# 1/rms on ScalarE and GpSimd in a two-layer encoder: ln and exp with one Newton step in place of three Newton steps on VectorE

## The chip, the core and the metric

The kernel runs on one core of a Trainium2 chip. The core has five engines that run side by side, each through its own instructions in order: TensorE (PE, matrix products, results in PSUM), VectorE (DVE), ScalarE (ACT), GpSimd (POOL) and SyncE (SP, which here issues most DMAs). They meet at semaphores only. The metric is the device time of one execution in microseconds (us), the median of several runs.

## The reference

Two layers, each with four groups of attention heads beside each other, an output projection, and an MLP with squared ReLU; 1024 tokens, model width 1024, all in float32. What matters here is every place that divides by a root mean square:

```python
def rms_norm(x, g):
    y = x * lax.rsqrt(jnp.mean(x * x, axis=-1, keepdims=True) + EPS)
    return y * g
...
for l in range(DEPTH):
    h = rms_norm(x, norm1_g[l])                 # before the input projection
    ...
    q = rms_norm(cq, q_norm_g) @ w_uq           # group A: latents of 192 and
    c = rms_norm(ckv, kv_norm_g)                #   of 128 columns
    w = p[:, :, 0] - lam * p[:, :, 1]           # group B: difference of two softmaxes
    o = rms_norm(o, subln_g)                    #   norm of each head's output
    mix = concat([rms_norm(y_a), y_b, rms_norm(y_c), rms_norm(y_d)])
    x = x + mix @ w_out[l]
    h = rms_norm(x, norm2_g[l])
    x = x + jnp.square(relu(h @ w_up[l])) @ w_down[l]
return rms_norm(x, final_norm_g)
```

Group C also adds a sink, exp(sink − max), to each softmax denominator.

## The kernel before, in words

Activations lie transposed: a tile has 128 features in its partitions and tokens along its rows, so a token's sum of squares runs over partitions. Each float32 product is made of three passes over rounded halves (`wh`, `wl` for weights; `xh`, `xl`, `far` for activations): lines 220 to 222. ACT writes the high half (L194), DVE or POOL the low one by subtraction (L188, the helper `tt`, which records every elementwise operation of two tensors).

A norm works like this. ACT squares, DVE sums tiles, PE multiplies by ones (L261), which puts the sums of 128 tokens into one PSUM column, so 1024 tokens are a tile of 128x8. `rstd_cols` scales it and adds EPS (`ms`, L263), `rsqrt_cols` makes 1/rms of it (`rs_r`, with `rs_t` as scratch): an integer guess (L247) and three Newton steps of three small DVE operations each (L249, L188, L251), ten operations in a row that each need the one before. The columns go back into rows either by products with the identity (`spread_here`, L297) or by a PE transpose (L270), a copy (L272), a store to DRAM (`drows`) and a broadcast load (`rows_of`, `spread`).

The order of one layer: input projection of group B's columns; attention B (`attn_b`) with the projections of A's latents and of group D woven in; attention D with the projection of C and `latent_up`; attention C; attention A with parts of the output projection; the MLP (`mlp_up`, `mlp_down`). A norm that isn't needed at once is a tail, a generator that `tick` advances by a step between steps of the main work. `proj_latent` (L664 on) collects sums of squares of the latents in `sq0` to `sq2`, and at its end makes two 1/rms, one after the other, in the middle of attention B. `attn_b` softmaxes two score tiles for each block of queries: `p` is read out of PSUM by a custom DVE operation with a running maximum `nm` (L809), ACT takes the exponential (L812); then the coefficient `cb` = z0 · (−lambda) / z1 (L893, L894) scales the second tile (ACT, L896), POOL adds the two, PE transposes the sum (L843) and multiplies it with v (L831, L832). `sub_norm` is B's norm, `mix_group` that of D, C and A, `final` the last one, run for each half of the tokens.

Instructions are put in order by a scheduler that goes by its own model of durations; in the MLP, PE's order alone is the code's.

Of the kernel before, what the change touches and what calls it, by code (L numbers as in the profile page):

```python
# [15 lines left out]
I32 = mybir.dt.int32  # L16
AF = mybir.ActivationFunctionType
ALU = mybir.AluOpType
# [127 lines left out]
class Trunk:  # L146
# [94 lines left out]
    def rsqrt_cols(self, ms):  # L241

        nc = self.nc
        n = ms.shape[1]
        r = self.cp.tile([P, n], F, tag="rs_r", name="rs_r")
        t = self.cp.tile([P, n], F, tag="rs_t", name="rs_t")
        nc.vector.tensor_scalar(r.bitcast(I32), ms.bitcast(I32), -0.5, 1597463007.0, ALU.mult, ALU.add)  # L247
        for _ in range(3):
            nc.vector.scalar_tensor_tensor(out=t, in0=r, scalar=-0.5, in1=r, op0=ALU.mult, op1=ALU.mult)  # L249
            self.tt(t, t, ms)  # L250
            nc.vector.scalar_tensor_tensor(out=r, in0=t, scalar=1.5, in1=r, op0=ALU.add, op1=ALU.mult)  # L251
        return r

    def rstd_cols(self, sq, count, rhs, tag="mm"):

        nc = self.nc
        g = rhs.shape[1]
        n = sq.shape[1] // P
        ps = self.bank(tag, [P, n * g])
        for t in range(n):  # L260
            nc.tensor.matmul(ps[:, t * g:(t + 1) * g], sq[:, t * P:(t + 1) * P], rhs, start=True, stop=True)  # L261
        ms = self.cp.tile([P, n * g], F, tag="ms", name="ms")
        nc.vector.tensor_scalar(ms, ps, 1.0 / count, EPS, ALU.mult, ALU.add)  # L263
        return self.rsqrt_cols(ms)
# [36 lines left out]
    def setup(self):  # L301
        nc, d = self.nc, self.d
        tile = lambda shape, name, dt=F: self.const.tile(shape, dt, name=name)
# [360 lines left out]
    def proj_latent(self, l, one, xs, rb, tabs, lat, krd, rows_out):  # L664
# [3 lines left out]
        squares = [self.col("sq%d" % i, 8) for i in range(3)]  # L668
# [20 lines left out]
        self.tt(q, q, squares[1], ALU.add)  # L689
        for m, count in ((q, 192), (k, 128)):  # L690
            nc.vector.tensor_scalar(m, m, 1.0 / count, EPS, ALU.mult, ALU.add)
            rows_out.append(self.rows_of(self.rsqrt_cols(m)))
# [175 lines left out]
    def attn_b(self, l, t, qb, kb, vb, out):  # L868
# [3 lines left out]
        def head(h2):  # L872
# [15 lines left out]
            def probs(qt):  # L888
                ps = []
                for c in range(2):  # L890
# [3 lines left out]
                nc.vector.scalar_tensor_tensor(out=c, in0=z[0][:, qt:qt + 1], scalar=self.nlam[:, l:l + 1], in1=c,  # L894
                                               op0=ALU.mult, op1=ALU.mult)
# [12 lines left out]
    def sub_norm(self, y, rz, out):  # L908
# [6 lines left out]
        r = self.rstd_cols(sq, 64, self.pairs)  # L915
# [150 lines left out]
    def attn_c(self, l, qc, kc, vc, ys):  # L1066
# [3 lines left out]
        for kv in range(2):  # L1070
# [6 lines left out]
            for g in range(2):  # L1077
# [16 lines left out]
                self.tt(z, z, es, ALU.add)  # L1094
# [21 lines left out]
    def mix_group(self, mix, k0, ys, g, eng=None):  # L1116
# [3 lines left out]
        r = self.rstd_cols(acc, 256, self.ones[:, 0:1])  # L1120
# [373 lines left out]
```

## Time and profile before

| | |
|---|---|
| runs of the kernel, us | 2724.05, 2724.58, 2730.74 (median 2724.58) |
| profiled execution: its span, us (the page gives no other time of it) | 2735.0 |
| mean granted PE clock in it | 0.966 of full speed |
| 1/rms in a run | 20, so 200 small operations on DVE |
| tables loaded by ACT | 1, at the start, 1.28 us |
| exponentials of dense attention (L812) | 192, mean 1147 ns |

A profile is one execution recorded instruction by instruction. Its page gives busy time for each engine; a list of waits says which instruction stood idle until which other one had ended; the timeline shows single instructions. A row reads: line of the code, engine, operation, tile written <- tiles read, shape and type. Times in a timeline are from the span's start. "PEld" is TensorE's loading of weights, which overlaps its products. A window's row gives the time of each engine in that stretch, the granted clock, the DMA engines' busy share and GB/s.

### The profile page before, as it was taken

How to read it: one execution, taken by the hardware profiler on the slowest of the kernel's cores; microseconds unless marked ns; L12 is line 12 of the kernel's file. 1: busy time of each engine (PE TensorE's matmuls, PEld its weight loads, DVE VectorE, ACT ScalarE, POOL GpSimd, SP SyncE). 2: the span in 40 equal slices, each digit the busy share in tenths (PEclk: the TensorE clock that was granted, in tenths of full speed). 3: DMA queues.
4: the chain of work that ended last, by engine and by line, in shares of the span. 5: the costliest groups of instructions: out<-in, count | busy, mean ns of one | idle time of the engine just before them, and what ended most of it. 6: DMA issues, size and time to landing. Idle time of an engine off the chain costs nothing.

```text
span 2735.0 us, 37689 instructions
## 1 busy us (share of the span) xinstructions
PE 2559.4 (94%) x12298; PEld 2112.1 (77%) x12298; DVE 2006.5 (73%) x3560; ACT 1434.5 (52%) x2555; POOL 1138.4 (42%) x762
## 2 busy tenths in 40 slices
PE   8989988999899999999999899799998999999997
PEld 6778866787678887888877687677876788878886
DVE  7787767884966769778567777588749666688776
ACT  4667756673534445444427676566735444444444
POOL 2555641201345554555435556322013455545552
PEclk9989999999999999999998899999999999999998
DMA  5534597322144457444254335963221444664431
GB/s 173 168 103 128 155 272 227 105 88 74 35 147 146 158 181 254 151 131 128 94 160 120 110 113 157 273 218 86 78 70 34 159 159 145 219 222 150 138 101 62
DMA packets 191667, 389.19 MB, mean 142 GB/s; under 512 B 23840, under 2 KB 33008, under 8 KB 191472
## 3 DMA queue, kind: packets, MB, share of 16 engines
q1 hardware_dynamic: 177648, 361.62, 43.1%
q10 hardware_dynamic: 13824, 25.17, 2.6%
q8 instruction: 97, 1.59, 0.2%
q14 instruction: 98, 0.80, 0.1%
HBM read 263.29 MB, written 123.41 MB: 141 GB/s over the span
## 4 chain that ended last, share of the span: by engine, by line
PE 68%; DVE 14%; DMA 7%; ACT 4%; issue 4%; POOL 1%; SPq 0%; DVEq 0%; ACTq 0%; POOLq 0%
PE u L220 8%; PE u L222 8%; PE u L221 8%; PE mm L220 5%; PE p L220 5%; PE p L221 5%; PE p L222 5%; PE mm L221 5%; PE mm L222 5%; PE sb L807 3%; DVE p L809 2%; DVE part L188 2%; PE tr L843 2%; ACT p L812 2%; DVE ptl L188 1%
## 5 line engine op out<-in xcount | busy, mean ns | idle before, releaser
L188 POOL TENSOR_TENSOR wl<-raw,wh 128x512 fp32r<-128x512 f32 x448 | 638.2, 1425 | 703.7 <-ACT wh L194 681.5
L194 ACT ACTIVATE wh<-raw 128x512 fp32r<-128x512 f32 x448 | 281.4, 629 | 580.6 <-PE u L221 317.9
L188 POOL TENSOR_TENSOR wl<-ws,wh 128x512 fp32r<-128x512 f32 (+1 forms) x120 | 150.5, 1256 | 473.4 <-ACT wh L194 465.5
L220 PE MATMUL u<-far,wh 128*128 128x512 f32 x768 | 302.3, 394 | 8.1 <-ACT ev L1240 5.9
L188 DVE TENSOR_TENSOR raw<-raw 128x512 f32<-128x512 f32 x256 | 227.5, 894 | 103.8 <-DMA raw<-in_w_up 51.8
L222 PE MATMUL u<-far,wl 128*128 128x512 f32 x768 | 301.2, 392 | 2.7 <-POOL wl L188 2.7
L221 PE MATMUL u<-far,wh 128*128 128x512 f32 x768 | 301.6, 393 | 0.2 <-DVE far L188 0.2
L188 DVE TENSOR_TENSOR ptl<-tr,pth 128x512 fp32r<-128x512 f32 (+2 forms) x384 | 238.4, 628 | 70.2 <-ACT pth L194 69.1
L812 ACT ACTIVATE p<-p,nm 128x1024 f32<-128x1024 f32 x192 | 220.2, 1147 | 97.6 <-DVE nm L809 95.1
L194 ACT ACTIVATE pth<-tr 128x512 fp32r<-128x512 f32 (+2 forms) x384 | 205.5, 547 | 117.7 <-PE tr L843 67.1
L220 PE MATMUL p<-far,wh 128*128 128x512 f32 x640 | 253.0, 395 | 8.0 <-DVE ev L188 8.0
L222 PE MATMUL p<-far,wl 128*128 128x512 f32 x640 | 252.0, 394 | 1.2 <-POOL wl L188 1.2
L221 PE MATMUL p<-far,wh 128*128 128x512 f32 x640 | 252.1, 394 | 0.0
L807 PE MATMUL sb<-stack 96*128 96x512 f32 x640 | 219.8, 426 | 26.4 <-DVE nm L809 25.7
L188 DVE TENSOR_TENSOR far<-act,far 128x512 fp32r<-128x512 f32 x224 | 205.4, 946 | 14.6 <-ACT far L194 14.6
L188 POOL TENSOR_TENSOR p<-p 128x1024 f32<-128x1024 f32 x64 | 154.4, 2416 | 143.8 <-ACT p L896 130.4
L220 PEld LDWEIGHTS u<-far,wh 128*128 128x128 f32 x768 | 145.9, 190 | 40.6 <-ACT ev L1240 7.2
L222 PEld LDWEIGHTS u<-far,wl 128*128 128x128 f32 x768 | 145.8, 190 | 34.2 <-POOL wl L188 3.5
L220 PE MATMUL mm<-xh,wh 128*128 128x512 f32 x416 | 170.6, 410 | 0.9 <-DVE both L188 0.5
L221 PEld LDWEIGHTS u<-far,wh 128*128 128x128 f32 x768 | 145.7, 190 | 30.9 <-DVE far L188 0.5
L222 PE MATMUL mm<-xh,wl 128*128 128x512 f32 x416 | 167.9, 404 | 0.1
L221 PE MATMUL mm<-xl,wh 128*128 128x512 f32 x416 | 167.6, 403 | 0.0
(243 smaller groups left out, 6141.2 us busy)
## 6 DMA issues: line engine op xcount, KB each, us to landing
act<-acts SPq DMA_DIRECT2D x224, 256.0 KB
raw<-in_w_up SPq DMA_DIRECT2D x128, 256.0 KB
acts<-ev SPq DMA_DIRECT2D x128, 256.0 KB
raw<-in_w_down SPq DMA_DIRECT2D x128, 256.0 KB
acts<-ev ACTq DMA_DIRECT2D x96, 256.0 KB
ws<-in_w_in SPq DMA_DIRECT2D x76, 256.0 KB
rz<-drows SPq DMA_DIRECT2D x40, 256.0 KB
stack<-kd SPq DMA_DIRECT2D x32, 256.0 KB
```

The source lines that it names most:

```text
L188: (eng or self.nc.vector).tensor_tensor(out=out, in0=a, in1=b, op=op)
L194: nc.scalar.activation(hi, src, AF.Copy)
L220: mm(ps, w[0], x[0][:, sl], start=start, stop=False)
L221: mm(ps, w[0], x[1][:, sl], start=False, stop=False)
L222: mm(ps, w[1], x[0][:, sl], start=False, stop=stop)
L807: self.nc.tensor.matmul(ps, q[:, qt * P:(qt + 1) * P], k[:, sl], start=i == 0, stop=i == len(passes) - 1)
L809: self.nc.vector.tensor_tensor_reduce(out=p[:, sl], in0=ps, in1=self.zero[:, 0:1].bitcast(F).broadcast_to([P, 512]), scale=-scale, scalar= ...
L812: self.nc.scalar.activation(p, p, AF.Exp, bias=nm[:, 1:2], scale=-1.0, accum_out=z)
L843: nc.tensor.transpose(t[:, k * 256 + i * P:k * 256 + (i + 1) * P], p[:, (j * 2 + k) * P:(j * 2 + k + 1) * P], self.ident)
```

## The change

`rsqrt_cols` takes the logarithm and exp(−0.5 · ln) on ACT and then one Newton step, on the engine that is asked for: DVE (three operations), or POOL (four, since it has them in another form). POOL is asked for in `sub_norm`, in the mix norms of D and C, and for the latents; DVE stays for the first norm of a layer, A's mix norm, the MLP's norm and the final one. The latents' two sums stand in one tile of 128x16, summed and scaled by POOL, with one 1/rms, one transpose and one store. B's coefficient becomes a TENSOR_SCALAR with one tensor and two per-partition scalars. In attention C, POOL adds the sink to z. A set of ACT's tables that has ln and exp is named at the start.

```diff
-    def rsqrt_cols(self, ms):
+    def rsqrt_cols(self, ms, eng=None):
         r = self.cp.tile([P, n], F, tag="rs_r", name="rs_r")
         t = self.cp.tile([P, n], F, tag="rs_t", name="rs_t")
-        nc.vector.tensor_scalar(r.bitcast(I32), ms.bitcast(I32), -0.5, 1597463007.0, ALU.mult, ALU.add)
-        for _ in range(3):
-            nc.vector.scalar_tensor_tensor(out=t, in0=r, scalar=-0.5, in1=r, op0=ALU.mult, op1=ALU.mult)
-            self.tt(t, t, ms)
-            nc.vector.scalar_tensor_tensor(out=r, in0=t, scalar=1.5, in1=r, op0=ALU.add, op1=ALU.mult)
+        nc.scalar.activation(r, ms, AF.Ln)
+        nc.scalar.activation(r, r, AF.Exp, scale=-0.5)
+        if eng is not None:
+            self.tt(t, r, r, eng=eng)
+            self.tt(t, t, ms, eng=eng)
+            eng.tensor_scalar(t, t, -0.5, 1.5, ALU.mult, ALU.add)
+            self.tt(r, r, t, eng=eng)
+            return r
+        nc.vector.scalar_tensor_tensor(out=t, in0=r, scalar=-0.5, in1=r, op0=ALU.mult, op1=ALU.mult)
+        self.tt(t, t, ms)
+        nc.vector.scalar_tensor_tensor(out=r, in0=t, scalar=1.5, in1=r, op0=ALU.add, op1=ALU.mult)
         return r
...
     def setup(self):
+        nc.scalar.preload_act_table_set("natural_log_exp_and_others")
...
     def proj_latent(...):
-        squares = [self.col("sq%d" % i, 8) for i in range(3)]
+        ms, more = self.col("sq0", 16), self.col("sq1", 8)
+        squares = [ms[:, 0:8], more, ms[:, 8:16]]
...
-        self.tt(q, q, squares[1], ALU.add)
+        self.tt(q, q, more, ALU.add, nc.gpsimd)
         for m, count in ((q, 192), (k, 128)):
-            nc.vector.tensor_scalar(m, m, 1.0 / count, EPS, ALU.mult, ALU.add)
-            rows_out.append(self.rows_of(self.rsqrt_cols(m)))
+            nc.gpsimd.tensor_scalar(m, m, 1.0 / count, EPS, ALU.mult, ALU.add)
+        both = self.rows_of(self.rsqrt_cols(ms, nc.gpsimd))
+        rows_out.extend([both[0:8], both[8:16]])
...
     def attn_b(...):
-                nc.vector.scalar_tensor_tensor(out=c, in0=z[0][:, qt:qt + 1], scalar=self.nlam[:, l:l + 1], in1=c,
-                                               op0=ALU.mult, op1=ALU.mult)
+                nc.vector.tensor_scalar(c, c, z[0][:, qt:qt + 1], self.nlam[:, l:l + 1], ALU.mult, ALU.mult)
...
     def sub_norm(...):
-        r = self.rstd_cols(sq, 64, self.pairs)
+        r = self.rstd_cols(sq, 64, self.pairs, eng=nc.gpsimd)
...
     def attn_c(...):
-                self.tt(z, z, es, ALU.add)
+                self.tt(z, z, es, ALU.add, nc.gpsimd)
...
     def mix_group(...):
-        r = self.rstd_cols(acc, 256, self.ones[:, 0:1])
+        r = self.rstd_cols(acc, 256, self.ones[:, 0:1], eng=None if eng else self.nc.gpsimd)
```

The scheduler orders attention anew: of PE's 12,092 products about 960 stand elsewhere, all in attention; in the MLP PE's order is the same. Lines of the new kernel differ from the old by −1 at first and by up to +8 later (L809 is L817, L812 is L820, L896 is L903).

First place: DVE in attention B of layer 0, where the latents' sums are complete. The rows `ISA p,nm` are the softmax reads of a score tile, `sq_829` and `sq_831` the sums, `rs_r` the two 1/rms. Before:

```order
L272 COPY rows<-mm 8x128
L893 RECIPROCAL cb<-z_1388 128x1
L188 TENSOR_TENSOR sq_829<-sq_829,sq_830 128x8
L894 SCALAR_TENSOR_TENSOR cb<-z_1387,nlam,cb 128x1
L809 ISA p,nm<-sb,zero 128x512
L809 ISA nm 128x1
L691 TENSOR_SCALAR sq_829<-sq_829 128x8
L809 ISA p,nm<-sb,zero,nm 128x512
L809 ISA nm 128x1
L247 TENSOR_SCALAR rs_r<-sq_829 128x8
L247 TENSOR_SCALAR rs_r<-sq_831 128x8
```

and at the same place now:

```order
L277 COPY rows<-mm 8x128
L901 RECIPROCAL cb<-z_1383 128x1
L902 TENSOR_SCALAR cb<-cb,z_1382,nlam 128x1
L817 ISA p,nm<-sb,zero 128x512
L817 ISA nm 128x1
L817 ISA p,nm<-sb,zero,nm 128x512
L817 ISA nm 128x1
L197 SCALAR_TENSOR_TENSOR both<-part,par,both 64x512
L817 ISA p,nm<-sb,zero 128x512
```

The sums, their scaling and the chain of both 1/rms are gone from between the softmax reads. They are now on POOL, between its additions of the two softmaxes (`p<-p`), the tables of the rotation (`tabc`, `tabs`) and low halves (`both`); before, its rows there were

```order
L188 TENSOR_TENSOR tabc<-tabc,rb 128x1024
L188 TENSOR_TENSOR tabs<-tabs,rb 128x1024
L188 TENSOR_TENSOR p<-p 128x1024
L188 TENSOR_TENSOR both<-part,both 48x512
L188 TENSOR_TENSOR p<-p 128x1024 x2
```

and now they are

```order
L187 TENSOR_TENSOR tabc<-tabc,rb 128x1024
L187 TENSOR_TENSOR sq_825<-sq_825,sq_826 128x8
L187 TENSOR_TENSOR tabs<-tabs,rb 128x1024
L187 TENSOR_TENSOR p<-p 128x1024
L187 TENSOR_TENSOR both<-part,both 48x512
L698 TENSOR_SCALAR sq_825<-sq_825 128x8
L187 TENSOR_TENSOR p<-p 128x1024
L187 TENSOR_TENSOR rs_t<-rs_r 128x16
L187 TENSOR_TENSOR rs_t<-rs_t,sq_825 128x16
L251 TENSOR_SCALAR rs_t<-rs_t 128x16
L187 TENSOR_TENSOR rs_r<-rs_r,rs_t 128x16
```

Between the scaling and the four Newton operations stand ACT's ln and exp; in ACT's order they are placed among exponentials (L820) and high halves of transposed softmaxes (`pth`):

```order
L820 ACTIVATE p,z_1382<-p,nm 128x1024
L903 ACTIVATE p<-p,cb 128x1024
L193 ACTIVATE pth<-tr 128x512 x2
L246 ACTIVATE rs_r<-sq_825 128x16
L820 ACTIVATE p,z_1383<-p,nm 128x1024
L757 ACTIVATE pvt<-pv 64x512
L247 ACTIVATE rs_r<-rs_r 128x16
```

On PE, the transpose of the joined norms stands at row 567 of its order; before, the two transposes stood at row 558, and what now lies ahead of it besides is 14 transposes of `p`, 3 products of scores and 5 products with v.

Second place: DVE at the norm of layer 0's MLP, where `raw` are sums of weight blocks and `far` low halves of activations. Before:

```order
L263 TENSOR_SCALAR ms<-mm 128x8
L247 TENSOR_SCALAR rs_r<-ms 128x8
L249 SCALAR_TENSOR_TENSOR rs_t<-rs_r 128x8
L188 TENSOR_TENSOR raw<-raw 128x512
L188 TENSOR_TENSOR rs_t<-rs_t,ms 128x8
L198 SCALAR_TENSOR_TENSOR far<-x_7141,par,far 128x512
L188 TENSOR_TENSOR raw<-raw 128x512
L251 SCALAR_TENSOR_TENSOR rs_r<-rs_t,rs_r 128x8
L249 SCALAR_TENSOR_TENSOR rs_t<-rs_r 128x8
L188 TENSOR_TENSOR rs_t<-rs_t,ms 128x8
```

and now:

```order
L268 TENSOR_SCALAR ms<-mm 128x8
L187 TENSOR_TENSOR raw<-raw 128x512
L197 SCALAR_TENSOR_TENSOR far<-x_7093,par,far 128x512
L254 SCALAR_TENSOR_TENSOR rs_t<-rs_r 128x8
L187 TENSOR_TENSOR raw<-raw 128x512
L187 TENSOR_TENSOR rs_t<-rs_t,ms 128x8
L256 SCALAR_TENSOR_TENSOR rs_r<-rs_t,rs_r 128x8
```

The guess and two of three steps are gone; the same two `raw` and one `far` stand among what is left.

Third place: ACT at the first half of the final norm, where L1455 squares a block of x and L1456 scales it; ln and exp are new there:

```order
L1456 ACTIVATE x_19775<-x_19775,par 128x512
L1455 ACTIVATE ev<-x_19856 128x512
L246 ACTIVATE rs_r<-ms 128x4
L1456 ACTIVATE x_19856<-x_19856,par 128x512
L247 ACTIVATE rs_r<-rs_r 128x4
L193 ACTIVATE wh<-raw 128x512
```

ln stands behind a square and exp behind a scaling of x. In the second half nothing stands between or behind them.

More of the change, by code (lines that the diff above doesn't have):

```diff
@@ L15 @@
 R = mybir.dt.float32r
-I32 = mybir.dt.int32
 AF = mybir.ActivationFunctionType
@@ L246, in rsqrt_cols, with rstd_cols @@
         t = self.cp.tile([P, n], F, tag="rs_t", name="rs_t")
-        nc.vector.tensor_scalar(r.bitcast(I32), ms.bitcast(I32), -0.5, 1597463007.0, ALU.mult, ALU.add)
-        for _ in range(3):
-            nc.vector.scalar_tensor_tensor(out=t, in0=r, scalar=-0.5, in1=r, op0=ALU.mult, op1=ALU.mult)
-            self.tt(t, t, ms)
-            nc.vector.scalar_tensor_tensor(out=r, in0=t, scalar=1.5, in1=r, op0=ALU.add, op1=ALU.mult)
+        nc.scalar.activation(r, ms, AF.Ln)
[9 more added lines that the diff above has]
+        nc.vector.scalar_tensor_tensor(out=r, in0=t, scalar=1.5, in1=r, op0=ALU.add, op1=ALU.mult)
         return r
-    def rstd_cols(self, sq, count, rhs, tag="mm"):
+    def rstd_cols(self, sq, count, rhs, tag="mm", eng=None):
         nc = self.nc
@@ L263, in rstd_cols @@
         nc.vector.tensor_scalar(ms, ps, 1.0 / count, EPS, ALU.mult, ALU.add)
-        return self.rsqrt_cols(ms)
+        return self.rsqrt_cols(ms, eng)
     def rows_of(self, col, grid=False):
```

## The prediction

> **What bounds the kernel now.** I read the page's busy shares first.
>
> ```profile
> PE 2559.4 (94%) x12298; PEld 2112.1 (77%) x12298; DVE 2006.5 (73%) x3560; ACT 1434.5 (52%) x2555; POOL 1138.4 (42%) x762
> ```
>
> TensorE (PE) is the bound, 94% busy; what a change can win is its idle time, 175.6 us (2735.0 less 2559.4), and the time it runs below full clock. So the second view is the list of waits, for PE alone. Columns: total us, times, longest.
>
> ```profile
> PE sb L807 <- DVE nm L809: 25.7, 23, 5.4
> ...
> PE mm L297 <- DVE rs_r L251: 6.4, 2, 4.1
> ...
> PE u L297 <- DVE rs_r L251: 5.7, 2, 3.5
> ...
> PE mm L270 <- DVE rs_r L251: 3.2, 3, 2.0
> ```
>
> Three of these rows wait for the last Newton step of a 1/rms (rs_r). The first, the scores of dense attention waiting for VectorE (DVE) to empty a PSUM bank, is the longest of all PE's waits. Third view: how long the small DVE operations of the changed lines take (min/median/max ns).
>
> ```profile
> L249 DVE SCALAR_TENSOR_TENSOR rs_t<-rs_r x60: 135/166/2368, 30.6 to 2723.1; 128x8 f32<-128x8 f32 x42, 128x16 f32<-128x16 f32 x12, 128x4 f32<-128x4 f32 x6
> ...
> L691 DVE TENSOR_SCALAR sq<-sq x4: 171/1046/2274, 136.5 to 1509.5; 128x8 f32<-128x8 f32 x4
> ...
> L893 DVE RECIPROCAL cb<-z x64: 142/159/167, 97.2 to 1691.7; 128x1 f32<-128x1 f32 x64
> ...
> L894 DVE SCALAR_TENSOR_TENSOR cb<-z,nlam,cb x64: 201/219/2427, 99.2 to 1692.6; 128x1 f32<-128x1 f32 x64
> ```
>
> Operations of 0.2 us sometimes take 2.4 us, but never the reciprocal (167 ns at most in 64). The timeline says when: here the latents' norms in layer 1's attention B, with GpSimd (POOL) beside them. Columns: start, length, engine, what; idle before it.
>
> ```profile
> 1509.42 2.36 POOL L188 TENSOR_TENSOR p<-p 128x1024 f32<-128x1024 f32 x1
> 1509.54 2.27 DVE L691 TENSOR_SCALAR sq<-sq 128x8 f32<-128x8 f32 x1
> ...
> 1511.06 0.58 PE L831 MATMUL pv<-pth,v 128*128 128x256 f32 x1 [1.37 <-ACT pth L194]
> ...
> 1513.21 2.36 POOL L188 TENSOR_TENSOR tabs<-tabs,rb 128x1024 f32<-128x1024 f32 x1
> 1513.28 2.31 DVE L188 TENSOR_TENSOR rs_t<-rs_t,sq 128x8 f32<-128x8 f32 x1
> ...
> 1517.07 1.40 PE L807 MATMUL sb<-stack 96*128 96x512 f32 x2 [5.43 <-DVE nm L809]
> ...
> 1519.14 1.15 ACT L812 ACTIVATE p<-p,nm 128x1024 f32<-128x1024 f32 x1 [7.66 <-DVE nm L809]
> ...
> 1525.20 0.38 PE L270 MATMUL mm<-ident,rs_r 128*8 128x128 f32 x1 [2.04 <-DVE rs_r L251]
> ```
>
> A tiny DVE operation that starts under a POOL operation ends with it: 1509.54 + 2.27 and 1509.42 + 2.36 both give 1511.8; the tabs pair both ends at 1515.6. Meanwhile the softmax reads (L809) queue behind it on DVE, PE runs out of scores and idles 1.37 + 5.43 + 2.04 = 8.8 us. Layer 0 has the same place:
>
> ```profile
> 165.81 0.79 PE L807 MATMUL sb<-stack 96*128 96x512 f32 x1 [1.38 <-DVE nm L809]
> ...
> 167.56 0.58 PE L831 MATMUL pv<-pth,v 128*128 128x256 f32 x1 [0.96 <-ACT pth L194]
> ...
> 169.76 1.28 POOL L188 TENSOR_TENSOR both<-part,both 48x512 fp32r<-48x512 f32 x1
> ...
> 172.95 0.79 PE L807 MATMUL sb<-stack 96*128 96x512 f32 x1 [4.80 <-DVE nm L809]
> ...
> 177.18 0.63 PE L270 MATMUL mm<-ident,rs_r 128*8 128x128 f32 x2
> ```
>
> That is 7.1 us for PE ahead of its transpose of the two norms at 177.2; POOL's split of 48 rows ends at 171.0 behind a row of longer operations. The Trainium skill, "SBUF — State Buffer", section "SBUF: two separate sides", has a rule for this: DVE and GpSimd share one port pair, whoever starts first holds it for a whole instruction, and a DVE operation with two SBUF inputs or in a two-port mode must have it. The trace agrees, with the 2.27 us above.
>
> **The change part by part.** All durations are of one profiled execution with a span of 2735.0 us; the runs' median, 2724.58, is 10.4 us less (the page gives no time around the span), so I sum changes to the span and take them off the median.
>
> *Latents' norms (both layers).* Before, they put 23 small operations on DVE: an addition, two L691, and two times ten of the 1/rms. After, none: POOL does an addition, two scalings and four Newton operations, ScalarE (ACT) ln and exp. The softmax reads then follow each other on DVE, and the idle of 8.8 + 7.1 = 16 us loses its cause. Two transposes, two copies and two stores on SP become one each. What is late next is POOL: its last scaling stands behind the 48-row split that ended at 171.0, then comes a 2.4 us operation, then the four Newton steps once exp is there: 171.0 + 0.2 + 2.4 + 4 × 0.24 = 174.6 at the earliest. ACT's ln stands behind softmax work (the order above), so it, too, may wait for the scaling. PE's transpose stood at 177.2 with 7.1 us of idle ahead of it; without that, and with the 14 transposes of p, three score products and five products with v that now stand ahead of it (some 6 us), PE comes to it at about 176. One us of slack is little, and ACT's idle of 7.66 may leave a rest. I take three quarters, **−12**; bounds −4 (a quarter) to −16.
>
> *Coefficient of B, 64 times.* The trace shows the two-tensor form waiting: 64 × (434 mean − 219 median) = 13.8 us of DVE.
>
> ```profile
> L894 DVE SCALAR_TENSOR_TENSOR cb<-z,nlam,cb 128x1 f32<-128x1 f32 x64 | 27.8, 434 | 1.2
> ```
>
> The new TENSOR_SCALAR has one tensor operand of 128x1 and two per-partition scalars. Nearest rows: the 128x1 reciprocal never waits; the 128x8 TENSOR_SCALAR of L691 does. I go by the shape, 128x1. Most of the 13.8 us lies where DVE has slack (73% busy); I take **−2**, bounds 0 to −13.8. The Trainium skill, "VectorE: DVE Perf Modes", section "Mode 2×_2P", lets a single-source SBUF operation use both read ports when the outermost dimension is even: that fits L691's 2.27 us, and one element isn't even; if this form took both ports all the same, this term would be 0.
>
> *Norm of the MLP (both layers).* PE's 6.4 us in two waits. Six of nine Newton operations go, at a pitch of 0.2 us:
>
> ```profile
> 752.49 0.17 DVE L249 SCALAR_TENSOR_TENSOR rs_t<-rs_r 128x8 f32<-128x8 f32 x1
> 752.69 0.17 DVE L188 TENSOR_TENSOR rs_t<-rs_t,ms 128x8 f32<-128x8 f32 x1
> ...
> 753.71 3.78 PE L297 MATMUL mm<-ident,rs_r 128*128 128x128 f32 x16 [4.14 <-DVE rs_r L251]
> ```
>
> 6 × 0.2 = 1.2 us each. ln and exp lie beside the DVE operations that still stand between ms and the first product (a raw and a far). **−2.4**, bounds 0 to −6.4.
>
> *Final norm, twice.*
>
> ```profile
> 2701.79 0.63 ACT L1448 ACTIVATE ev<-x 128x512 f32<-128x512 f32 x1 [0.33 <-DVE x L188]
> ...
> 2702.45 0.72 ACT L1449 ACTIVATE x<-x,par 128x512 f32<-128x512 f32 x1
> ...
> 2704.60 1.29 PEld L297 LDWEIGHTS u<-ident,rs_r 128*128 128x128 f32 x8 [3.59 <-DVE rs_r L251]
> ...
> 2721.53 0.16 DVE L263 TENSOR_SCALAR ms<-u 128x4 f32<-128x4 f32 x1 [1.14 <-PE u L261]
> ...
> 2723.71 2.08 PE L297 MATMUL u<-ident,rs_r 128*128 128x128 f32 x8 [2.22 <-DVE rs_r L251]
> ```
>
> The next row is ACT's smallest exp, the price of ln and of exp:
>
> ```profile
> L352 ACT ACTIVATE lam_e<-lam_e x2: 186/194/203, 23.1 to 24.3; 128x2 f32<-128x2 f32 x2
> ```
>
> The first now waits on ACT: ln stands behind ev, exp behind x (the order above): 2702.4 + 0.2 + 0.7 + 0.2 + three at 0.2 = 2704.1 for 2704.6, −0.5. In the second nothing is ahead: 2.2 us become 0.2 (ms) + 2 × 0.2 + 3 × 0.2 + some 0.1 of hand-overs = 1.3, −0.9. **−1.4**, bounds +1 to −3.
>
> *First norm of each layer:* six operations less before the spread, but PE is busy there; PE's products of the spread stand five rows earlier. I take **−2**, bounds 0 to −4.
>
> *Clock.* Half-clock follows the latents' idle:
>
> ```profile
> 136.00:205.00 69.00, 59.26 (x292) 48.56 (x291) 57.49 (x147) 45.68 (x72) 36.88 (x20) 0.85 0.38 104
> ...
> 1504.00:1572.00 68.00, 57.87 (x279) 46.90 (x279) 52.37 (x138) 41.16 (x65) 35.13 (x19) 0.85 0.37 109
> ```
>
> A mean of 0.85 over 69 us is 20 us at half speed, so up to 10 us of work per layer; part of it precedes the norms. I take **−3**, bounds 0 to −10.
>
> *What is added.* POOL gets 54 small operations, which the trace doesn't show; from
>
> ```profile
> L188 POOL TENSOR_TENSOR wl<-ws,wh 128x512 fp32r<-128x512 f32 x96 | 131.4, 1371 | 207.2 <-ACT wh L194 199.4 <-ACT pth L194 3.4 <-DMA stack<-kb 3.0
> ...
> L188 POOL TENSOR_TENSOR wl<-ws,wh 128x256 fp32r<-128x256 f32 x24 | 19.1, 795 | 266.2 <-ACT wh L194 266.1
> ...
> L188 POOL TENSOR_TENSOR p<-p 128x1024 f32<-128x1024 f32 x64 | 154.4, 2416 | 143.8 <-ACT p L896 130.4 <-PE tr L843 6.4 <-PE mm L220 3.2
> ```
>
> 256 columns cost 0.58 us, so 8 or 16 cost about 0.24 by the line through both (0 to 0.8): 13 us of POOL, 42% busy. Eight of them (z plus sink, attention C) stand ahead of a DVE reciprocal, which holds up DVE's softmax reads until POOL is through. I take **+2.5** for both, bounds 0 to +43 (18 waits, rival 3). ACT gets 36 operations of 0.19: 7 us at 52%, hidden beside PE but in the places above. The norms of B, C and D lie beside other heads' work; I cost them at nothing, and 1 us of PE each (10) if that cover fails.
>
> Sum: −12 − 2 − 2.4 − 1.4 − 2 − 3 + 2.5 = −20.3: span 2715, and **2704.3** against the median.
>
> **Rivals.**
> 1. *The idle was the whole story, and more:* all 16 us, 10 of the clock, 10 of the coefficient, 3 + 1.4 + 2 of the rest: −42, **2682**; halfway −30, **2695**. For it: DVE is 57.49 of 69 us busy in that window and ACT waited with it. Against: POOL's queue.
> 2. *Given back at once:* POOL's 54 operations hold the port against DVE in turn (54 × 0.24 = 13 us), or PE's transpose waits for POOL's Newton steps as it did for DVE's (2 × 3 us), or both: −20 + 6, + 13 or + 19, so 2711, **2718** or 2724. The Trainium skill's port rule, cited above from "SBUF — State Buffer", would have it so. For: POOL runs back to back there. Against: DVE's reads of PSUM, which feed PE, show no such waits. Belongs here too: all of attention is ordered anew, and two layers of like order differ by chance by 5 us of PE busy time in one window:
>
> ```profile
> 341.00:410.00 69.00, 56.34 (x311) 47.19 (x311) 42.68 (x115) 37.42 (x95) 29.06 (x20) 0.95 0.97 271
> ...
> 1709.00:1777.00 68.00, 51.05 (x267) 41.51 (x265) 38.91 (x104) 34.45 (x87) 22.90 (x15) 0.92 0.95 272
> ```
>
> 3. *Slower:* in-order engines wait for POOL. Ten Newton chains end in a PE transpose, eight additions in a DVE reciprocal; each can stand behind a 2.4 us POOL operation: 18 × 2.4 = +43, less 20, **2748**. It turns slower by more than 0.3% from 12 of the 18 on (28.8 − 20 = 8.8). For: PE and DVE don't overtake. Against: the additions of z lie in attention C, where POOL adds no softmaxes.
> 4. *It doesn't do what it says:* ln and exp each reload ACT's table, as at the start:
>
> ```profile
> 0.73 1.28 ACT L194 ACT_TABLE_LOAD   x1 [0.73 <-PEq L1482]
> ```
>
> 36 × 1.28 = 46 us on ACT, half of it on the path: −20 + 23, **2728**. Each program has a single load, so this is nearly excluded.
>
> **How the numbers follow.** Forecast (2704, within 2696 to 2712) 0.45; rival 1 0.16; rival 2 0.24; rival 3 0.13; rival 4 0.02. Range 2686 to 2730: it leaves out half of rival 1's far end and most of rival 3. A measurement can tell some 0.3% from no change, 8.2 us. Faster (under 2716.4): 0.45 + 0.16 + a third of rival 2 = 0.69. Slower (over 2732.8): 0.11. Same: 0.20.
>
> **What would show it.** Right: no small DVE operation over 1 us in attention B; TENSOR_SCALAR cb at about its median throughout; PE's wait for nm well under 25.7 us and no idle over 3 us at the latents' norms; DVE's busy time down by 60 us or more; the MLP's waits for rs_r at 4 us for 6.4. Wrong: waits of PE or ACT on POOL's rs_r or sq, DVE's rz waiting for POOL's z, a cb that still takes 2.4 us, or PE idle of the old size at other places of attention.

## The result, and the profile after

The changed kernel takes **2702.86 us** (median of 4 runs, 2701.14 to 2705.85) where the kernel before, in runs beside it, takes 2727.66 (2724.05 to 2731.97). The ratio is 0.9901, with a 95% interval of 0.9881 to 0.9921. The prediction was 2704.3 within 2686 to 2730. The profiled execution has a span of 2698.9 us for 2735.0. The profile of before was a long one, so its difference of 36 us is more than the 24.8 us between the medians; below, stages are compared with care for that.

The page's busy shares after:

```profile
PE 2545.4 (94%) x12296; PEld 2109.5 (78%) x12296; DVE 1944.6 (72%) x3368; ACT 1438.1 (53%) x2591; POOL 1151.6 (43%) x816
```

DVE lost 62 us of busy time (2006.5 to 1944.6), while PE lost 14 (2559.4 to 2545.4): PE's idle time fell from 175.6 to 153.5 us. PE's waits say which idle time went (total us, times, longest):

```profile
PE sb L815 <- DVE nm L817: 12.8, 19, 2.4
...
PE mm L302 <- DVE rs_r L256: 5.6, 2, 3.3
...
PE u L302 <- DVE rs_r L256: 4.1, 2, 2.8
...
PE tr L851 <- POOL p L187: 2.6, 1, 2.6
```

The wait for the softmax reads halved, from 25.7 us to 12.8, and its longest went from 5.4 to 2.4 us. The MLP's wait for `rs_r` fell by 0.8 us, the final norm's by 1.6. The last row, a transpose that waited for POOL's sum of two softmaxes, stood at 0.4 us before. The durations of the changed lines (min/median/max ns), from two answers by tile:

```profile
L901 DVE RECIPROCAL cb<-z x64: 140/159/166, 98.7 to 1660.9; 128x1 f32<-128x1 f32 x64
L902 DVE TENSOR_SCALAR cb<-cb,z,nlam x64: 251/272/275, 100.7 to 1661.6; 128x1 f32<-128x1 f32 x64
```

```profile
L187 POOL TENSOR_TENSOR rs_t<-rs_r x10: 201/210/217, 175.1 to 1857.9; 128x16 f32<-128x16 f32 x6, 128x8 f32<-128x8 f32 x4
L251 POOL TENSOR_SCALAR rs_t<-rs_t x10: 202/204/209, 175.7 to 1858.5; 128x16 f32<-128x16 f32 x6, 128x8 f32<-128x8 f32 x4
L187 POOL TENSOR_TENSOR rs_r<-rs_r,rs_t x10: 201/220/222, 176.0 to 1858.8; 128x16 f32<-128x16 f32 x6, 128x8 f32<-128x8 f32 x4
L254 DVE SCALAR_TENSOR_TENSOR rs_t<-rs_r x8: 151/170/1218, 31.1 to 2686.8; 128x8 f32<-128x8 f32 x6, 128x4 f32<-128x4 f32 x2
```

The coefficient never waits now (275 ns at most of 64; 2427 before), though its median is 0.05 us longer. In all of attention no DVE operation on 16 columns or fewer takes over 0.8 us any more; before, single ones took up to 2.4. A Newton operation on POOL takes 0.20 to 0.22 us.

Now the place that the prediction put first, the latents' norms in layer 1's attention B, by the timeline (start, length; in brackets the idle time before it and what ended it):

```profile
1500.64 0.20 POOL L698 TENSOR_SCALAR sq<-sq 128x8 f32<-128x8 f32 x1
1500.92 4.67 POOL L187 TENSOR_TENSOR p<-p 128x1024 f32<-128x1024 f32 x2
...
1501.13 0.20 ACT L246 ACTIVATE rs_r<-sq 128x16 f32<-128x16 f32 x1
...
1502.27 0.20 ACT L247 ACTIVATE rs_r<-rs_r 128x16 f32<-128x16 f32 x1
...
1503.32 1.54 PE L851 MATMUL tr<-ident,p 128*128 128x128 f32 x6 [2.59 <-POOL p L187]
...
1505.55 0.21 POOL L187 TENSOR_TENSOR rs_t<-rs_r 128x16 f32<-128x16 f32 x1
...
1505.84 0.22 POOL L187 TENSOR_TENSOR rs_t<-rs_t,sq 128x16 f32<-128x16 f32 x1
...
1506.15 0.21 POOL L251 TENSOR_SCALAR rs_t<-rs_t 128x16 f32<-128x16 f32 x1
1506.44 0.22 POOL L187 TENSOR_TENSOR rs_r<-rs_r,rs_t 128x16 f32<-128x16 f32 x1
...
1507.39 0.38 PE L275 MATMUL mm<-ident,rs_r 128*16 128x128 f32 x1
```

Ln starts 0.3 us after POOL's scaling is through, exp a good microsecond later behind the scaling of `p`; then the Newton step stands behind two additions of `p` on POOL until 1505.6. That costs PE nothing: the transpose at 1507.39 has no idle before it. The one wait left, 2.59 us, is for the first of the same two additions. In layer 0, 2.40 and 0.85 us are left, both for `nm`:

```profile
166.40 0.80 PE L815 MATMUL sb<-stack 96*128 96x512 f32 x1 [2.40 <-DVE nm L817]
...
175.47 0.50 PE L815 MATMUL sb<-stack 96*128 96x512 f32 x1 [0.85 <-DVE nm L817]
```

So the idle of 8.8 + 7.1 = 16 us is now 2.6 + 3.3 = 5.8. What the whole of attention B made of it shows in a table by stretches, from the first score product of B to its last one (its last products with v follow some 30 us later, beside attention D). Columns: the window and its length; busy us of PE, PE's weight loads, DVE, ACT and POOL with their counts; the mean granted clock; the share of the DMA engines; GB/s. Before, layer 0 and layer 1:

```profile
83.30:332.90 249.60, 235.14 (x1230) 196.31 (x1229) 199.21 (x503) 178.56 (x284) 141.46 (x81) 0.94 0.44 127
1426.60:1688.80 262.20, 242.36 (x1223) 199.34 (x1222) 203.05 (x501) 177.89 (x284) 145.10 (x83) 0.92 0.43 124
```

and after:

```profile
85.80:322.70 236.90, 226.25 (x1183) 187.27 (x1182) 179.28 (x459) 174.57 (x280) 137.74 (x86) 0.96 0.42 124
1418.00:1655.00 237.00, 227.59 (x1205) 190.90 (x1204) 180.44 (x461) 176.00 (x283) 141.74 (x89) 0.96 0.43 127
```

The stretches are 12.7 and 25.2 us shorter, but not all of that is won. First, 47 and 18 of PE's products have left the stretch and are done behind it: in layer 0 the next stretch, attention D, is 6.4 us longer, in layer 1 attention D and C are 2.3 and 5.0 us longer and A 5.7 shorter. Second, the clock: 0.94 and 0.92 became 0.96, which over these lengths is 5.5 and 11.5 us of full-speed work more (249.60 × 0.06 − 236.90 × 0.04 and 262.20 × 0.08 − 237.00 × 0.04). A part of that has only moved: in the stretch ahead of B the clock was 1.00 in both layers, and it is 0.96 (0 to 85.8 us) and 0.98 (1343.3 to 1418.0 us) now, which gives back some 5 us. Third, PE's idle: 14.5 to 10.7 us and 19.8 to 9.4 us (length less PE's busy time).

### The profile page after: what moved, and what is told of

The parts are those of the page before. It is cut to its first block, busy times and chain, and to the rows that moved or that the text cites. A ratio compares the mean times of both kernels' runs of the same rounds, so it can differ in the third digit from the quotient of the medians.

```text
span 2698.9 us, 37585 instructions
## 1 busy us (share of the span) xinstructions
PE 2545.4 (94%) x12296; PEld 2109.5 (78%) x12296; DVE 1944.6 (72%) x3368; ACT 1438.1 (53%) x2591; POOL 1151.6 (43%) x816
## 4 chain that ended last, share of the span: by engine, by line
PE 73%; DVE 13%; DMA 5%; ACT 5%; issue 3%; POOL 1%; SPq 0%; DVEq 0%; ACTq 0%; POOLq 0%
PE u L219 8%; PE u L221 8%; PE u L220 8%; PE mm L219 6%; PE mm L220 5%; PE mm L221 5%; PE p L219 5%; PE p L220 5%; PE p L221 5%; PE sb L815 3%; DVE p L817 2%; DVE part L187 2%; PE tr L851 2%; ACT p L820 2%; DVE ptl L187 1%
## 5 line engine op out<-in xcount | busy, mean ns | idle before, releaser
L820 ACT ACTIVATE p<-p,nm 128x1024 f32<-128x1024 f32 x192 | 220.2, 1147 | 77.3 <-DVE nm L817 72.8
L815 PE MATMUL sb<-stack 96*128 96x512 f32 x640 | 217.6, 422 | 13.1 <-DVE nm L817 12.8
L187 POOL TENSOR_TENSOR p<-p 128x1024 f32<-128x1024 f32 x64 | 153.5, 2402 | 110.8 <-ACT p L903 103.0
L851 PE MATMUL tr<-ident,p 128*128 128x128 f32 x1024 | 163.2, 278 | 8.8 <-DVE ptl L187 6.0
```

Of the source, the lines that this page charges most:

```text
L187: (eng or self.nc.vector).tensor_tensor(out=out, in0=a, in1=b, op=op)
L815: self.nc.tensor.matmul(ps, q[:, qt * P:(qt + 1) * P], k[:, sl], start=i == 0, stop=i == len(passes) - 1)
L820: self.nc.scalar.activation(p, p, AF.Exp, bias=nm[:, 1:2], scale=-1.0, accum_out=z)
L851: nc.tensor.transpose(t[:, k * 256 + i * P:k * 256 + (i + 1) * P], p[:, (j * 2 + k) * P:(j * 2 + k + 1) * P], self.ident)
```

## The experiments

Each kernel of the table below ran several times beside the kernel before, whose median was 2730 to 2733 us in these runs (2728 beside the changed kernel itself); ratios are to it, and 0.1% is 2.7 us. The first eight rows take the change apart into three parts: the **latents** (joined, ln and exp, Newton step and sums on GpSimd), the **coefficient**, and the **other norms** with the sink's addition on GpSimd. "Idle" is the sum of PE's waits of over 0.8 us around the latents' norms (163 to 178 and 1500 to 1525 us), layer 0 and 1. B is the length of its two stretches, from first to last score product. "Rest" is the span less the time from the first score of B to the MLP's first product in both layers: first norms, MLP norms, MLPs, final norm. The last three columns are worked out from each profile's single execution.

| kernel | ratio to before, 95% interval | idle | B | rest |
|---|---|---|---|---|
| before | 1 | 7.1, 8.8 | 249.7, 262.2 | 1477.1 |
| coefficient alone | 0.9947 (0.9928 to 0.9965) | 8.9, 7.0 | 251.1, 249.1 | 1478.5 |
| latents alone | 0.9972 (0.9954 to 0.9990) | 3.4, 2.3 | 238.8, 239.4 | 1477.2 |
| other norms alone | 0.9955 (0.9935 to 0.9974) | 7.6, 3.8 | 249.6, 244.6 | 1472.5 |
| coefficient and latents | 0.9956 (0.9942 to 0.9970) | 3.2, 2.6 | 236.9, 238.9 | 1478.8 |
| coefficient and other norms | 0.9980 (0.9963 to 0.9998) | 8.9, 10.2 | 249.4, 264.1 | 1471.7 |
| latents and other norms | 0.9920 (0.9895 to 0.9945) | 4.2, 4.2 | 240.5, 240.1 | 1474.1 |
| all three (the change) | 0.9901 (0.9881 to 0.9921) | 3.3, 2.6 | 236.9, 237.0 | 1473.5 |
| before, lead 42 | 0.9987 (0.9974 to 1.0000) | 7.7, 8.3 | 252.1, 254.4 | 1477.3 |
| change, lead 42 | 0.9929 (0.9912 to 0.9947) | 4.3, 2.8 | 243.1, 241.8 | 1471.7 |
| change, lead 38 | 0.9910 (0.9891 to 0.9928) | 2.1, 2.4 | 238.0, 239.1 | 1476.9 |
| change, Newton on VectorE | 0.9965 (0.9949 to 0.9982) | 6.0, 3.1 | 250.7, 238.9 | 1474.3 |
| change, coefficient in two columns | 0.9936 (0.9913 to 0.9958) | 5.9, 2.5 | 240.4, 241.2 | 1471.4 |
| change without a Newton step | 0.9900 (0.9879 to 0.9922) | 1.9, 2.6 | 234.5, 234.4 | 1478.0 |

**The coefficient alone, and the change without it.** The edit, made in the kernel before, and undone in the changed one:

```diff
-nc.vector.scalar_tensor_tensor(out=c, in0=z[0][:, qt:qt + 1], scalar=self.nlam[:, l:l + 1], in1=c, ...)
+nc.vector.tensor_scalar(c, c, z[0][:, qt:qt + 1], self.nlam[:, l:l + 1], ALU.mult, ALU.mult)
```

> The kernel before with one edit: B's coefficient is a TENSOR_SCALAR of one tensor operand and two per-row scalars, in place of the SCALAR_TENSOR_TENSOR. Theory: the 64 coefficient operations stop waiting for GpSimd (mean from about 0.45 us to 0.27 us, none over 0.5 us), which takes some 11 to 14 us of waiting out of VectorE's queue in attention B; a part of it reaches TensorE, so the time falls by 2 to 8 us; the latents' idle of 7 to 9 us per layer stays as it was. Rival A (hidden: ScalarE and TensorE have work beside it): 0 within 2 us, although the operations are short. Rival B (a chance order): the operations are short and the time moves by several us in a stage that has no coefficient in it.

> The kernel after the change with the coefficient's SCALAR_TENSOR_TENSOR back. Theory: its mean rises from 0.27 to 0.40 us or more, with single ones over 2 us, and the time rises by 2 to 8 us above the changed kernel. Rival A (hidden): within 2 us of it. Rival B (a chance order): more than 10 us above it, or below it by over 3 us.

The waits came and went as the theory said, in both kernels. With the old form back in the changed kernel, its row in the answer by tile reads:

```profile
L902 DVE SCALAR_TENSOR_TENSOR cb<-z,nlam,cb x64: 197/220/2426, 100.6 to 1671.9; 128x1 f32<-128x1 f32 x64
```

The time is less plain: 0.9947 for the coefficient alone, 14 us, is more than the theory's 8, and a part of it lies in stages without a coefficient (attention D and A of layer 1 are 4.8 and 4.5 us shorter, C of layer 0 is 6.5 longer), as rival B has it. Some 10 us of it are clock: these ten runs have a granted clock of 0.9700 in the mean, the kernel before 0.9665 over its 80 runs beside the experiments (2730 × 0.0335 − 2714 × 0.0300). The changed kernel with the old coefficient gives up 5 us (0.9920 for 0.9901, intervals that overlap). With the coefficient alone, the latents still hold PE up. This is the timeline of the kernel with that edit, in layer 0's attention B:

```profile
166.11 2.34 POOL L188 TENSOR_TENSOR tabs<-tabs,rb 128x1024 f32<-128x1024 f32 x1
166.22 2.34 DVE L249 SCALAR_TENSOR_TENSOR rs_t<-rs_r 128x8 f32<-128x8 f32 x2
...
168.42 2.34 POOL L188 TENSOR_TENSOR p<-p 128x1024 f32<-128x1024 f32 x1
168.51 2.35 DVE L188 TENSOR_TENSOR rs_t<-rs_t,sq 128x8 f32<-128x8 f32 x2
170.82 1.32 DVE L251 SCALAR_TENSOR_TENSOR rs_r<-rs_t,rs_r 128x8 f32<-128x8 f32 x2
170.84 1.28 POOL L188 TENSOR_TENSOR both<-part,both 48x512 fp32r<-48x512 f32 x1
...
173.82 0.79 PE L807 MATMUL sb<-stack 96*128 96x512 f32 x1 [8.86 <-DVE nm L809]
```

Three pairs of Newton operations follow each other on DVE, and each pair ends with the POOL operation beside it: 168.56 against 168.45, 170.86 against 170.76, 172.14 against 172.12. The score reads come behind them, and PE idles 8.86 us.

**The latents alone, and the change without them.** The first puts the change's `proj_latent` and its `rsqrt_cols` (for this use alone) into the kernel before; the second puts the old ones into the changed kernel. Of the first edit, the lines that differ from the change (`rsqrt_new` is the change's `rsqrt_cols`, beside the old one):

```diff
...
-rows_out.append(self.rows_of(self.rsqrt_cols(m)))
+both = self.rows_of(self.rsqrt_new(ms, nc.gpsimd))
+rows_out.extend([both[0:8], both[8:16]])
```

> The kernel before with one edit: the latents' two norms are joined, with ln and exp on ScalarE and one Newton step and the sums on GpSimd; all other norms keep three Newton steps on VectorE and the coefficient keeps its SCALAR_TENSOR_TENSOR. Theory: the idle of TensorE at the latents' norms falls from 7.1 and 8.8 us to about 3 us each and the clock recovers beside it, so the time falls by 10 to 16 us, the most of all parts; the coefficient still waits, mean 0.40 to 0.50 us. Rival A (the coefficient is what counts): less than 4 us. Rival B (a chance order): the idle at the latents goes but the stages behind attention B give back all but 3 us.

> The kernel after the change with the latents' norms as they were (two, each three Newton steps on VectorE). Theory: the idle of 7 to 9 us per layer is back, the time rises by 10 to 16 us above the changed kernel, to 2713 to 2719 us, and the coefficient stays at 0.27 us. Rival A (the other norms and the coefficient carry it): within 4 us of the changed kernel. Rival B (no part carries it alone, a chance order of attention does): more than 20 us above, or below the changed kernel.

The mechanism shows in both: the idle falls to 3.4 and 2.3 us with the edit and is back at 8.9 and 10.2 without. So does attention B, by the same windows for the kernel with the latents alone:

```profile
85.70:324.60 238.90, 226.35 (x1184) 187.15 (x1184) 185.36 (x468) 173.98 (x278) 135.65 (x81) 0.96 0.41 123
1431.50:1670.90 239.40, 229.37 (x1205) 191.78 (x1204) 183.69 (x468) 174.32 (x279) 138.74 (x84) 0.96 0.43 124
```

But the time is 0.9972, 8 us, less than the 10 to 16 expected, because the stages behind B give back part of it, as its rival B had it: 46 and 18 of B's products are done behind B, and from the end of B to the MLP's first product this kernel takes 384.8 and 380.8 us, where before takes 371.1 and 374.9. Taking the latents out of the changed kernel costs 21 us (0.9980 for 0.9901), more than the 10 to 16 expected and the number of its rival B, a chance order. The idle explains 13 of it (8.9 + 10.2 against 5.8); the other 8 are as much as an order alone moves below.

**The other norms alone.** Ln, exp and one Newton step everywhere but at the latents, the sink's addition on GpSimd, the coefficient as before. In the places of these norms it has the diff of the change, as

```diff
-r = self.rstd_cols(sq, 64, self.pairs)
+r = self.rstd_cols(sq, 64, self.pairs, eng=nc.gpsimd)
...
-self.tt(z, z, es, ALU.add)
+self.tt(z, z, es, ALU.add, nc.gpsimd)
```

> The kernel before with the other edits alone: ln, exp and one Newton step at the first, MLP and final norms and at attention's output norms, and the sink's addition on GpSimd; the latents' norms and the coefficient as before. Theory: the stages outside attention (first norm, MLP norm, final norm) fall by 5 to 9 us together, attention B stays at 249 us or more with 7 to 10 us of idle at the latents in each layer, so the time is 3 to 10 us below the kernel before, give or take the 4 to 8 us that an order alone is worth. Rival (these norms gain nothing, since their stages wait for other work): the stages outside attention within 2 us of before.

0.9955 is 12 us, at the far end of what was expected with its allowance. The stages outside attention give 4.6 of it (1477.1 to 1472.5), just short of the 5 expected. Over all kernels of the table but the one without a Newton step, "rest" is 1477.1 to 1478.8 with the old norms and 1471.4 to 1476.9 with the new, 4.5 us apart in the mean. The two groups don't overlap, though the new one spreads over 5.5 us. By stage the 4.5 us are 2.7 in the two MLPs, 1.6 in the final norm and 0.2 up to attention B. The idle at layer 1's latents fell to 3.8 us with nothing changed there, and B to 244.6 us where 249 or more was expected; there the order alone did it.

**The coefficient and the latents together.** Both edits above, in the kernel before.

> The kernel before with two edits: the latents' norms joined (ln, exp, one Newton step on GpSimd) and the coefficient with one tensor operand; the other norms keep three Newton steps. Theory: both stretches of attention B at 235 to 242 us as in the changed kernel, and only the 5 to 9 us of the other norms outside attention missing: 2708 to 2716 us. Rival (the order of attention in the changed kernel owes its gain to the other norms): a stretch of attention B at 249 us or more, and the time over 2720 us.

B is as short as in the changed kernel (236.9 and 238.9). The time, 2719.08 us (0.9956), misses the 2708 to 2716 expected. It is 15 us above that of the change (0.9901): the expected 5 to 9 of the other norms, and some 6 to 10 more in the later stages of attention (9.5 in the profiles).

**Order alone.** One number of the scheduler's, in the kernel before (42) and in the changed one (42, then 38), with no operation added or removed:

```diff
-NP, RB, RD, LB, LD = 6, (7, 8), (3, 2), 40, 50
+NP, RB, RD, LB, LD = 6, (7, 8), (3, 2), 42, 50
```

> The kernel before with one number of the order changed: the projections that fill attention B are given a lead of 42 in place of 40, and no operation is added or removed. It sizes what a new order by itself is worth. Theory (the operations of the change carry the gain): within 5 us of the kernel before, with 14 to 20 us of idle TensorE in each attention B as before. Rival (a chance order carries most of it): 10 us or more in either direction.

> The kernel after the change with the same one number, a lead of 42 in place of 40. Theory: within 5 us of the changed kernel, both stretches of attention B stay at 235 to 242 us. Rival (a chance order): 10 us or more above the changed kernel, one of the two stretches back at 250 us or more.

> The kernel after the change with the lead of attention B's fill at 38 in place of 40, no operation added or removed: a second new order of the same operations. Theory (the operations carry the gain, and an order alone is worth 4 to 10 us): 2700 to 2714 us, both stretches of attention B under 245 us, latents' idle under 5 us in each layer. Rival (the order that the change happened to get carries most of the gain): over 2720 us, with a stretch of attention B at 249 us or more.

An order alone moved the time by −3.5, +7.6 and +2.5 us; the second, with its B of 243.1 us, is past the 5 us and the 242 us that were expected. The changed operations keep their gain under all three orders (0.9901, 0.9929, 0.9910), and the old ones don't come near it (1 and 0.9987). Over the whole table, B takes 234.4 to 243.1 us in the eight kernels that have the latents joined on GpSimd and 244.6 to 264.1 in the five with the old ones. So the operations carry the gain, some 22 us by these means (0.9913 against 0.9994), and the order of the changed kernel as given is a good one by a few us.

**The Newton step on VectorE.** The changed kernel with the sums, the scaling and all Newton steps on DVE, ln and exp still on ACT:

```diff
-self.tt(q, q, more, ALU.add, nc.gpsimd)
+self.tt(q, q, more, ALU.add)
...
-both = self.rows_of(self.rsqrt_cols(ms, nc.gpsimd))
+both = self.rows_of(self.rsqrt_cols(ms))
```

> The kernel after the change with every norm's sums and Newton step on VectorE in place of GpSimd (ln and exp stay on ScalarE, the latents stay joined). Theory (VectorE's small operations wait for GpSimd, one after the other): six operations per layer at the latents wait up to 2.4 us each, so TensorE's idle there is 4 to 8 us per layer in place of about 2.5 to 3, and the time is 3 to 10 us above the changed kernel. Rival A (only the number of operations counts, and the joined form with ln and exp has few enough): within 2 us of the changed kernel. Rival B (GpSimd's long p additions ahead of the Newton step cost more than the port): 2 to 5 us below the changed kernel.

It gives up 17 us of the change's 27 (0.9965), more than the 3 to 10 expected. At layer 0's latents the step has only three operations on DVE. In the timeline of this kernel they are

```profile
165.36 2.30 DVE L254 SCALAR_TENSOR_TENSOR rs_t<-rs_r 128x16 f32<-128x16 f32 x1
...
168.20 1.77 DVE L187 TENSOR_TENSOR rs_t<-rs_t,sq 128x16 f32<-128x16 f32 x1
...
170.57 0.75 DVE L256 SCALAR_TENSOR_TENSOR rs_r<-rs_t,rs_r 128x16 f32<-128x16 f32 x1
```

and POOL has beside them

```profile
164.85 2.78 POOL L187 TENSOR_TENSOR tabs<-tabs,rb 128x1024 f32<-128x1024 f32 x1
167.59 2.34 POOL L187 TENSOR_TENSOR p<-p 128x1024 f32<-128x1024 f32 x1
170.02 1.27 POOL L187 TENSOR_TENSOR both<-part,both 48x512 fp32r<-48x512 f32 x1
```

All three end with POOL's operations (167.66 and 167.63; 169.97 and 169.93; 171.32 and 171.29), and PE's idle there is 4.64 + 1.37 us. Over both layers that place costs 3.3 us more than in the changed kernel (6.0 + 3.1 for 5.8); the rest of the 17 us lies elsewhere in attention, which no run here takes apart. Part of it may be order: layer 0's B is 13.8 us longer than in the changed kernel and holds 71 of PE's products more. Still, 17 us are twice the most that an order alone moved. Rival A is out: the smaller number of operations is not what wins alone, taking them off DVE counts.

**What keeps the coefficient from waiting.** The change with the coefficient made in two equal columns, of which the first is used:

```diff
-c = self.col("cb")
-nc.vector.reciprocal(c, z[1][:, qt:qt + 1])
+c = self.col("cb", 2)
+nc.vector.reciprocal(c, z[1][:, qt:qt + 1].broadcast_to([P, 2]))
...
```

> The kernel after the change with the coefficient made in two equal columns (128x2 in place of 128x1, the first is used), the same TENSOR_SCALAR. It asks what keeps the coefficient from waiting for GpSimd. Theory (one tensor operand and two per-row scalars do, whatever the width): none of the 64 over 0.4 us, and the time within 2 us of the changed kernel. Rival (the single column does; the 128x8 TENSOR_SCALARs on rows in SBUF did wait in the kernel before): single ones over 1 us, a mean of 0.35 us or more, and the time 2 to 8 us above the changed kernel.

The answer by tile for this kernel:

```profile
L901 DVE RECIPROCAL cb<-z x64: 143/161/169, 97.1 to 1667.9; 128x2 f32<-128x2 f32 x64
L902 DVE TENSOR_SCALAR cb<-cb,z,nlam x64: 267/289/2261, 99.0 to 1668.6; 128x2 f32<-128x2 f32 x64
```

The rival holds: the same instruction on two columns waits up to 2.26 us, and the 64 take 35.7 us in place of 17.2. The theory as put for this run, that the kinds of operands decide, falls. The time is 2713.72 us, 0.9936 for 0.9901: 9 us, with intervals that just overlap. Both ways of bringing the coefficient's waits back into the changed kernel thus cost time, 5 and 9 us, but little more than an order alone does.

**No Newton step.** The changed kernel with 1/rms by ln and exp alone, the Newton step left out:

```diff
 nc.scalar.activation(r, r, AF.Exp, scale=-0.5)
-if eng is not None:
-    self.tt(t, r, r, eng=eng)
-    ...
-nc.vector.scalar_tensor_tensor(out=t, in0=r, scalar=-0.5, in1=r, op0=ALU.mult, op1=ALU.mult)
-...
 return r
```

> The kernel after the change without any Newton step: 1/rms is ln and exp on ScalarE alone, the correction of their rounding is left out. It sizes what is left in these operations. Theory: three operations of VectorE or four of GpSimd go per norm; outside attention 1 to 4 us, at the latents up to 2 us per layer, so 0 to 8 us below the changed kernel (2695 to 2703 us), give or take what an order alone is worth. Rival A (the step is hidden already): within 2 us of the changed kernel outside attention, and the latents' idle at 2.5 to 3.5 us per layer as in it. Rival B (a new order costs more than the step): above 2706 us, with the surplus in attention.

Nothing is gained: 2705.20 us, 0.9900. Attention B is 2.5 us shorter in each layer, and attention D behind it longer by 6 and 8 us. The rest takes 4.5 us more, although PE no longer waits for `rs_r` at the MLP norms and the final norm is 2.6 us shorter. The two MLPs are 4.2 and 3.6 us longer, with PE's idle there the same within 1 us and a granted clock of 0.98 for 0.99; why the clock is lower is open. What is left in these operations doesn't show in the time.

## Why the prediction was right

**Latents, −12.** Right in mechanism and near in size: 16 us of idle became 5.8, so 10.2 went, and no wait there exceeds 2.6 us. In the eight kernels of the three parts, putting the latents in is worth 0.28, −0.09, 0.35 and 0.79%, in the mean 0.33% or 9 us, with the clock and a new order each time inside. My fear for the Newton step, one us of slack, did not come true: in layer 1 it came 3.1 us after exp behind two POOL additions, and PE still didn't wait, as it had other products. In two of the experiments it did, for 0.96 us (the change without the coefficient's new form) and 0.4 us (with two columns).

**Coefficient, −2.** The choice of shape over instruction was right, and the two-column run shows it: by L691's row the term would have been 0. The Trainium skill, "VectorE: DVE Perf Modes", section "Mode 2×_2P", lets one tensor use both read ports where its outermost non-unit dimension is even, or odd and equal in source and destination; a single column has nothing to split, and two columns do. One column is free and two wait, so the trace agrees. That one element "isn't even", as the prediction has it, is only half of that rule, and no run here has an odd width above one. There was luck in the choice, too: the reciprocal that spoke for the shape doesn't wait on eight columns either. In the changed kernel the reciprocals of the softmax sums read

```profile
L768 DVE RECIPROCAL rz<-z x24: 180/202/205, 142.9 to 1824.8; 128x8 f32<-128x8 f32 x24
L768 DVE RECIPROCAL rz<-za x8: 201/202/203, 521.4 to 1950.6; 128x8 f32<-128x8 f32 x8
```

and nine of these 32 began with at least 0.4 us of a POOL operation still to run (one at 203.42, under an addition of `p` from 202.40 to 204.80). In the kernel before, they took 205 ns at most as well. So that row was about the operation, and only the two-column run shows that the single column counts. The size may have been too small: the mean of the four pairs of kernels with and without it is 0.16%, 4 us (0.53, 0.16, −0.25 and 0.19, a spread that an order alone could make), and the two-column run says 9. These 64 operations lie between a softmax and the score reads of the next one, where DVE's "slack" isn't always there.

**MLP norm, −2.4, and final norm, −1.4.** PE's idle before the products, after:

```profile
746.12 3.53 PE L302 MATMUL mm<-ident,rs_r 128*128 128x128 f32 x16 [3.26 <-DVE rs_r L256]
```

and at the final norm, first half and second

```profile
2668.54 1.78 PEld L302 LDWEIGHTS u<-ident,rs_r 128*128 128x128 f32 x8 [2.89 <-DVE rs_r L256]
...
2687.45 2.08 PE L302 MATMUL u<-ident,rs_r 128*128 128x128 f32 x8 [1.32 <-DVE rs_r L256]
```

In the MLP 4.14 became 3.26 in layer 0, and layer 1 stayed at 2.3: 0.9 us for 2.4. One Newton operation still took 1.2 us there, and ln and exp now stand in the chain. The final norm's second half went from 2.22 to 1.32 us, the 0.9 forecast to the tenth; the first, by PE's weight load, from 3.59 to 2.89, 0.7 for a forecast of 0.5. With the first norms, forecast at −2, that makes −5.8 outside attention; the kernels show −4.5. What is missing is the first norms: PE's idle up to B in layer 0 is 9.6 to 10.0 us in every kernel of the table, with old norms or new, and in layer 1 it is 2.6 to 2.7 us in all but the kernel before, which has 4.0. The −2 there isn't borne out.

**Clock, −3.** Too small in the profiles: the mean over the span went from 0.966 to 0.969, which is 2735.0 × 0.034 − 2698.9 × 0.031 = 9.3 us of full-speed work, inside the bounds. The runs agree with the profiles: the kernel before has a clock of 0.9665 in the mean of its 80 runs beside the experiments, the changed one 0.9695 in its four, which is 9.0 us by the same sum.

**Added operations, +2.5.** POOL's small operations were 0.20 to 0.22 us for 0.24. One sign that I named for the wrong case did come: DVE's reciprocal of `z` waited for POOL's addition in three of eight places, by the list of DVE's waits (total, times, longest),

```profile
DVE rz L768 <- POOL z L187: 4.8, 3, 2.8
```

and no wait of PE or ACT for POOL's `rs_r` or `sq` is among the changed kernel's rows. Of rival 3 these 4.8 us on DVE are all there is. Rival 4 is out: one table load, as before.

**What was missing** is the size of giving back. Rival 2 had it as a case of its own, but in part it always happens: a shorter B leaves 18 to 47 of PE's products to the stages behind it, and an order of attention alone moved the time by 2.5 to 7.6 us. Missing, too, is what the other norms do inside attention, which the prediction put at nothing: with the sink's addition they are worth 0.45, −0.33, 0.52 and 0.55% in their four pairs of kernels, in the mean 8 us, and only 4.5 of it lie outside attention. No run takes the rest apart. The terms came to −20.3; by medians the change brings −24.8 us, and the operations some 22 over several orders. That the sum came within 1.4 us of the time is partly chance: the median of before that it was taken from was 3 us below that of the runs beside the changed kernel, the latents, the first norms and the MLP's wait brought less than forecast, the clock more, and the coefficient perhaps.

## What to carry to other kernels

A tiny VectorE operation on data in SBUF may last as long as the GpSimd operation beside it, so look at the maximum of a group and not only at its mean; where it stands ahead of reads that feed TensorE, give it a form that doesn't wait (here a single column with one tensor operand) or another engine. Take the idle time at the place, not VectorE's busy time, as the price: 62 us of busy time went, and 25 us of time. Before one part of a change is judged by its time alone, run the same operations in another order; here that alone was worth up to 8 us, as much as most parts.

## What the hardware showed that I had not expected

One column more makes the coefficient's operation wait: 275 ns at most for 128x1, 2261 for 128x2. The reciprocal never waited at any width that was run: 169 ns at most for the coefficient's one and two columns, 205 ns for the eight columns shown above.

The wait goes the other way too. In the changed kernel POOL's small addition of the latents' sums took three times its usual 0.2 us in both layers. In layer 0 DVE was in an operation with two SBUF inputs until 165.73:

```profile
165.13 0.66 POOL L187 TENSOR_TENSOR sq<-sq,sq 128x8 f32<-128x8 f32 x1
```

```profile
164.40 1.33 DVE L197 SCALAR_TENSOR_TENSOR both<-part,par,both 64x512 fp32r<-64x512 f32 x1 [1.17 <-ACT both L196]
```

In layer 1 the addition ends within 0.1 us of the same DVE operation, at 1494.4. The row of `tabs` at 164.85 above is the same: 2.78 us for some 2.36, behind that DVE operation, which in that kernel ran from 164.20 to 165.43. The Trainium skill, "SBUF — State Buffer", section "SBUF: two separate sides", says that whoever starts first holds the ports for the whole instruction; the trace agrees in both directions.
